# Splitting the weight slabs around a mixer by two transfers and a negation instead of by a subtraction on GpSimd

## The chip, the cores and the metric

The kernel runs on one core of one Trainium2 chip. The metric is the device time of one execution in microseconds (us); each kernel is executed several times and the median is compared. Engines are named as in the profile: PE is the matrix engine, PEld its weight loads, DVE the vector engine, ACT the scalar engine, POOL is GpSimd, and SP is the engine whose queue only starts transfers.

## The reference, cut to what matters

One layer in float32: a SwiGLU half-step, a mixer of two head groups (a gated convolution of width 31, and a linear recurrence), a second half-step, and a final norm, on 512 tokens of width 1024.

```
x = x + 1/2 * swiglu_ffn(rmsnorm(x), ffn1)        # 1024 -> 2816 -> 1024
x = x + hybrid_mixer(rmsnorm(x) @ w_in) @ w_out   # 1024 -> 2048, 1024 -> 1024
x = x + 1/2 * swiglu_ffn(rmsnorm(x), ffn2)
y = rmsnorm(x)
```

## The kernel before, in words

All large products run on PE in the type float32r. To keep the precision of float32, every operand is split into two float32r parts, hi (the value rounded) and lo (the value minus hi), and a product is three matmuls: hi times hi, hi times lo, lo times hi. The weights stream through as slabs of 128 partitions by 1024 columns (512 KB); there are 208 of them.

A slab passes through three stages, written as three functions. `slab_load` (L113) starts a transfer from SP's queue into a `raw` buffer (3 of them). `slab_hi` (L117) takes one of 5 buffers called `hl`, which hold both parts, and has ACT write the rounded copy (L119). `slab_lo` (L121) writes the lo part, raw minus hi (L133). It does so on DVE, or, for the slabs that are flagged `shared`, on POOL as long as a running estimate of POOL's work (`POOL_AHEAD`) is not over a limit: 72 of the 76 shared slabs go to POOL, 4 of them and the 132 others to DVE.

The program is a list of units, each the products on one slab. `run` (L159) goes through it; when it comes to the unit of slab n, it first emits the load up to slab n+5, the rounding up to n+3 and the lo part up to n+2 (`AHEAD`). A scheduler then places the instructions on the engines, and every engine takes its own in that order.

The units in order: gate and up products of the first half-step (weights stationary, 512 tokens, 24 matmuls a slab); its down products; the last 12 down slabs twice, for tokens 0 to 255 and then for 256 to 511 (`down_b_units`, two slabs of the first pass are kept for the second). Then the mixer: input products for half of the tokens at a time (`zc_units`, `rx_units`, `rg_units`, written to `pz`), the convolution as 248 operations on DVE (L503, L506), the recurrence (`lru`, L558), two multiplications of which are on POOL (L571, L590), a layer norm, and the output products (`out_units`). In between lie the gate and up products of the second half-step for tokens 0 to 255 (L712 to L716). All slabs from the second pass of the down products to these, 76 in number, are the shared ones. Each serves 256 tokens, so PE spends half as long on it as on a slab that serves 512. Before the units that need a new norm stands a `wait` (L679); the norm of two token tiles (`norm_chain`, L255) takes its sum of squares on ACT, two tiny operations on POOL (L218, L221), the scaling on DVE (L226), transposes on PE (L242), the rounding on ACT (L246) and the lo part on DVE (L252).

Of the kernel before, what the change touches and what calls it, by code (L numbers as in the profile page):

```python
# [8 lines left out]
F32 = mybir.dt.float32  # L9
F32R = mybir.dt.float32r  # L10
AF = mybir.ActivationFunctionType
ALU = mybir.AluOpType

P = 128
D = 1024
# [10 lines left out]
RAW_BUFS = 3  # L26
HL_BUFS = 5
ACT_BUFS = 19
AHEAD = (5, 3, 2)
POOL_CUT = 1  # L30
POOL_AHEAD = 1.0
DVE_AHEAD = 0.0
NY1 = 0
NY2 = 1
# [24 lines left out]
def layer_kernel(ctx: ExitStack, tc, x, gains, w_g1, w_u1, w_d1a, w_d1b, w_in,  # L59
                 chan, w_a, w_x, w_out, w_g2, w_u2, w_d2a, w_d2b, out):  # L60
    nc = tc.nc
    V, S, G, PE = nc.vector, nc.scalar, nc.gpsimd, nc.tensor

    cp = ctx.enter_context(tc.tile_pool(name="cp", bufs=1))
    wp = ctx.enter_context(tc.tile_pool(name="wp", bufs=4))
# [6 lines left out]
    def nm(s):  # L72
        uid[0] += 1
        return f"{s}_{uid[0]}"

    def const(shape, name, dt=F32):
        return cp.tile(shape, dt, name=name, tag=name)

# [1 line left out]
    xt = [const([P, D], f"xt{t}") for t in range(4)]  # L80
    h_hi = const([P, KT, T], "h_hi", F32R)
    h_lo = const([P, KT, T], "h_lo", F32R)
# [1 line left out]
    ones = const([P, P], "ones")  # L84
# [17 lines left out]
        nc.sync.dma_start(g, gains[i:i + 1, :].broadcast_to([P, D]))  # L102
        return g

# [1 line left out]
    clock = {"pe": 0.0, "dve": 0.0, "pool": 0.0}  # L106
    chains, convs, done = [], [], {}

    def dve(us):
        clock["dve"] = max(clock["dve"], clock["pe"] - 3.0) + us  # L110

    # slabs are loaded, then split into two parts of float32r
    def slab_load(st, src):  # L113
        st["raw"] = wp.tile([P, D], F32, name=nm("raw"), tag="raw", bufs=RAW_BUFS)
        nc.sync.dma_start(st["raw"], src)

    def slab_hi(st):  # L117
        st["hl"] = wp.tile([P, 2, D], F32R, name=nm("hl"), tag="hl", bufs=HL_BUFS)
        S.copy(st["hl"][:, 0, :], st["raw"])  # L119

    def slab_lo(st, shared):  # L121
        eng = V
        if shared:
            clock["pool"] = max(clock["pool"], clock["pe"])
            if clock["pool"] - clock["pe"] < POOL_AHEAD:
                eng = G
                clock["pool"] += 2.4
        if eng is V:
            dve(1.15)
        n = POOL_CUT if eng is G else 1  # L130
        for i in range(n):
            sl = slice(i * D // n, (i + 1) * D // n)
            eng.tensor_sub(st["hl"][:, 1, sl], st["raw"][:, sl],  # L133
                           st["hl"][:, 0, sl].bitcast(F32))

    def step_chains():
        for c in list(chains):
            with tc.high_priority(offset=c[0]):
                if next(c[1], None) is None:
                    chains.remove(c)  # L140

    def step_convs():
        while convs and clock["dve"] < clock["pe"] + DVE_AHEAD:
            with tc.high_priority(offset=PR_CONV):
                us = next(convs[0], None)
            if us is None:
                convs.pop(0)
            else:
                dve(us)
# [9 lines left out]
    def run(units, held):  # L159
        order = [i for i, x in enumerate(units) if x[0] is not None]  # L160
        st = [dict() for _ in order]
        put = [0, 0, 0]
        nth = 0
        for i, (src, shared, us, mm, evac) in enumerate(x[:5] for x in units):
            for stage, ahead in ((0, AHEAD[0]), (1, AHEAD[1]), (2, AHEAD[2])):
                most = HL_BUFS if i < held else len(order)
                while put[stage] < min(nth + ahead + 1, most):
                    q = put[stage]
                    if stage == 0:
                        slab_load(st[q], units[order[q]][0])  # L170
                    elif stage == 1:
                        slab_hi(st[q])
                    else:
                        slab_lo(st[q], units[order[q]][1])
                    put[stage] += 1
            hl = None
            if src is not None:
                hl = st[nth]["hl"]
                nth += 1
            mm(hl)  # L180
            clock["pe"] += us
            if us:
                step_chains()
                step_convs()
            if evac is not None:
                evac()

# [1 line left out]
    def mm_feat(ps, hl, t0, n):  # L189
        w = hl.rearrange("p s (k f) -> p s k f", k=KT)  # L190
        seq = [(0, h_hi), (0, h_lo), (1, h_hi)]
        for s, (a, h) in enumerate(seq):
            for k in range(KT):
                PE.matmul(ps, w[:, a, k, :], h[:, k, t0:t0 + n],  # L194
                          start=(s == 0 and k == 0), stop=(s == 2 and k == KT - 1))
# [5 lines left out]
            tc.keep_in_program_order(ins)  # L201
        return ins

    # a bank for the products beside the main ones
    def side_tile(name):
        if "free" in done:
            return pd.tile([P, T], F32, name=nm(name), tag="pd")
        return pp.tile([P, T], F32, name=nm(name), tag="pg")

# [1 line left out]
    def m4(name, dt=F32):  # L211
        return sp.tile([P, 4, HT], dt, name=nm(name), tag="act", bufs=ACT_BUFS)

# [58 lines left out]
        if key is not None:  # L272
            done[key] = True

# [1 line left out]
    def ffn_units(acts, j, wg, wu, parts, shared=False):  # L276
        box = {}

        def gate(t0, n, hl):
            if hl is not None:  # L280
                box["g"] = hl
            pg = pp.tile([P, T], F32, name=nm("pgate"), tag="pg")
            mm_feat(pg[:, :n], box["g"], t0, n)
            box["pg"] = pg

        def gate_out(t0, n):
            pg = box["pg"]
            sg = sp.tile([P, T], F32, name=nm("sg"), tag="sg", bufs=2)
            S.activation(sg[:, :n], pg[:, :n], AF.Silu)  # L289
            box["s"] = sg  # L290

        def up(t0, n, hl):
            if hl is not None:
                box["u"] = hl
            pu = pp.tile([P, T], F32, name=nm("pup"), tag="pg")
            mm_feat(pu[:, :n], box["u"], t0, n)
            box["pu"] = pu

        def up_out(t0, n):
            pu = box["pu"]  # L300
            sg = box["s"]
            act = acts[j]
            V.tensor_mul(sg[:, :n], pu[:, :n], sg[:, :n])  # L303
            S.copy(act[:, 0, t0:t0 + n], sg[:, :n])
            V.tensor_sub(act[:, 1, t0:t0 + n], sg[:, :n], act[:, 0, t0:t0 + n].bitcast(F32))  # L305
            dve(0.8 if n == 256 else 1.3)

        out_ = []
        for i, (t0, n) in enumerate(parts):
            us = 5.12 * n / 512  # L310
            out_.append((wg[j] if i == 0 else None, shared, us,
                         lambda hl, t0=t0, n=n: gate(t0, n, hl),
                         lambda t0=t0, n=n: gate_out(t0, n)))
            out_.append((wu[j] if i == 0 else None, shared, us,
                         lambda hl, t0=t0, n=n: up(t0, n, hl),
                         lambda t0=t0, n=n: up_out(t0, n)))
        return out_
# [6 lines left out]
            self[j] = new_act()  # L324
            return self[j]

# [1 line left out]
    def mm_tok(ps, ahi, alo, whi, wlo, first, last):  # L328
        PE.matmul(ps, ahi, whi, start=first, stop=False)  # L329
        PE.matmul(ps, ahi, wlo, start=False, stop=False)  # L330
        PE.matmul(ps, alo, whi, start=False, stop=last)  # L331
# [7 lines left out]
    def pd_tile():  # L339
        return pd.tile([P, 512], F32, name=nm("pd"), tag="pd")  # L340

    # down products of the first group of feature tiles, one half of the
    # output columns at a time, all tokens
    def down_a_units(wd, acts):
        box = {}

# [17 lines left out]
                 (lambda oh=oh: fin(oh)) if kp == NA // 2 - 1 else None)  # L364
                for oh in range(2) for kp in range(NA // 2)]

    # products of two token tiles with the full width of the output
    def pair_units(ws, order, kept, left, toks, scale, shared, after, again=False):
        box = {}
        n = len(order)  # L370
# [38 lines left out]
        order = [4, 5, 6, 7, 0, 1, 2, 3] if (YF0, YF1)[half] else list(range(8))  # L409
        return pair_units(w_out, order, {}, left, (2 * half, 2 * half + 1), 1.0, True, after)  # L410

# [1 line left out]
    def par(c, i):  # L413
        return ch[:, c, i:i + 1]

# [93 lines left out]
                    yield 0.4  # L509
        chains.append((PR_LN, layernorm(cv, half)))  # L510

    # mean over the channels, the same in every partition
    def channel_mean(v, box):
        ps2 = sp.tile([P, 2, HT], F32, name=nm("ps2"), tag="sg", bufs=2)
        V.tensor_add(ps2, v[:, 0:2, :], v[:, 2:4, :])
# [113 lines left out]
        V.tensor_scalar_mul(psp, q, 8.0)  # L629
        V.tensor_scalar_mul(nsp, q, -8.0)  # L630

# [1 line left out]
    row1 = sp.tile([1, P], F32, name="row1", tag="sg", bufs=2)  # L633
    V.memset(row1, 1.0)
    g1ps = [pd_tile() for _ in range(2)]
# [28 lines left out]
        return lambda: chains.append(  # L664
            (PR_NORM, norm_chain(toks, gains_of[n], f"h{n}{toks[0] // 2}")))

    # the same slabs once more, for the other half of the tokens
    def again_units(first, second):
        out_ = []
        for i, (_, _, us, mm, evac, _) in enumerate(second):  # L670
            box = {}
            first[i][5]["keep"] = box
            out_.append((None, False, us, lambda hl, mm=mm, box=box: mm(box.pop("hl")), evac))
        return out_
# [48 lines left out]
    for j in range(NB):  # L723
        u += ffn_units(b2, j, w_g2[NA:], w_u2[NA:], [ALL])

    # last down products and the final norm
    last = {}

    def final(k, hl):
# [100 lines left out]
```

## Time and profile before

| what | us |
|---|---|
| runs shown | 948.80 and 949.44, median 949.12 |
| span of the profiled execution | 945.9 |
| PE busy in the span | 907.8 |
| DVE busy | 475.1 |
| ACT busy | 368.6 |
| POOL busy | 210.8 |
| stretch 338 to 623 (the shared slabs): PE busy of 285 | 258.4 |
| the same stretch: DVE busy | 229.5 |

The span runs from the first to the last instruction of the profiled execution; it is 3.2 us shorter than the median of the runs, so the time of a kernel is read as its span and 3.2 us around it. A row of the groups gives the line, the engine, the operation, output and inputs by the program's names, shapes and count, then the total busy time, the mean in ns, and the idle time before. A row of a timeline gives start, duration, engine and instruction. A row of a table by stretches gives the length, then busy time and count of PE, PEld, DVE, ACT and POOL, then the granted PE clock, the share of the 16 transfer engines that is busy, and GB/s.

### The profile page before, as it was taken

To read this page: it belongs to the slowest core of one execution; us is meant where nothing else is said; L and a number is where in the kernel's file an instruction comes from. 1 tells how busy PE (TensorE), PEld (TensorE's weight loads), DVE (VectorE), ACT (ScalarE), POOL (GpSimd) and SP (SyncE) were. 2 spreads that over 40 slices of the span, in tenths; PEclk is the share of its full clock that TensorE was granted. 3 is DMA by queue.
4 is the path that set the end of the run, shared out by engine and by line. 5 is a ranking of instruction groups with operands and counts; after the bars stand their busy time and mean duration, and the time that the engine had idled before them with its cause. 6 is when DMAs were issued, how large, how long until landed. Compare 5 with 4: busy or idle time off the path is not lost.

```text
span 945.9 us, 11886 instructions
## 1 busy us (share of the span) xinstructions
PE 907.8 (96%) x4796; PEld 776.7 (82%) x4796; DVE 475.1 (50%) x677; ACT 368.6 (39%) x502; POOL 210.8 (22%) x120
## 2 busy tenths in 40 slices
PE   8999999999999999988889798999999999999997
PEld 6988888888888889888878697799988888888885
DVE  6533333333333433989999897555523333333224
ACT  6522221132222334466876554644511222223113
POOL 2000000000000038884856786700000000000001
PEclk9999999999999999998999899999999999999999
DMA  8322222322222344552433444445533222232202
GB/s 273 121 90 99 101 89 93 108 89 89 89 98 103 123 167 149 186 199 99 148 130 119 153 163 150 158 174 181 184 107 111 89 89 89 94 107 89 89 24 89
DMA packets 33401, 115.94 MB, mean 123 GB/s; under 512 B 4673, under 2 KB 4801, under 8 KB 33346
## 3 DMA queue, kind: packets, MB, share of 16 engines
q1 hardware_dynamic: 32770, 114.14, 34.8%
q10 hardware_dynamic: 576, 1.05, 0.3%
q8 instruction: 37, 0.61, 0.3%
q14 instruction: 18, 0.15, 0.0%
HBM read 113.07 MB, written 2.10 MB: 122 GB/s over the span
## 4 chain that ended last, share of the span: by engine, by line
PE 82%; DVE 13%; ACT 1%; DMA 1%; POOL 1%; issue 1%; SPq 0%; POOLq 0%; ACTq 0%; DVEq 0%
PE pgate L194 25%; PE pup L194 24%; PE pd L331 8%; PE pd L329 8%; PE pd L330 8%; PE pz L194 5%; DVE pc L506 4%; DVE xr L462 2%; PE pdl L331 1%; PE pdl L330 1%; PE pdl L329 1%; DVE th L595 1%; DVE xn L226 1%; DVE act L305 1%; DMA raw<-in_w_u 1%
## 5 line engine op out<-in xcount | busy, mean ns | idle before, releaser
L119 ACT CAST hl<-raw 128x1024 fp32r<-128x1024 f32 x208 | 217.7, 1048 | 330.6 <-PE pup L194 149.5
L133 DVE TENSOR_TENSOR hl<-raw,hl 128x1024 fp32r<-128x1024 f32 x136 | 168.2, 1237 | 290.3 <-ACT hl L119 290.3
L133 POOL TENSOR_TENSOR hl<-raw,hl 128x1024 fp32r<-128x1024 f32 x72 | 180.8, 2520 | 390.6 <-ACT hl L119 385.1
L194 PE MATMUL pgate<-h_hi,hl 128*128 128x512 f32 (+1 forms) x880 | 184.6, 352 | 0.8 <-ACT h_hi L246 0.8
L194 PE MATMUL pup<-h_hi,hl 128*128 128x512 f32 (+1 forms) x880 | 184.3, 351 | 0.3 <-DVE sg L303 0.3
L194 PEld LDWEIGHTS pgate<-h_hi,hl 128*128 128x128 f32 x880 | 145.0, 190 | 25.8 <-ACT h_hi L246 1.5
L194 PEld LDWEIGHTS pup<-h_hi,hl 128*128 128x128 f32 x880 | 144.9, 190 | 24.8 <-DVE sg L303 0.5
L329 PE MATMUL pd<-hl,act 128*128 128x512 f32 x304 | 118.4, 390 | 0.0
L331 PE MATMUL pd<-hl,act 128*128 128x512 f32 x304 | 118.3, 389 | 0.0
L330 PE MATMUL pd<-hl,act 128*128 128x512 f32 x304 | 118.3, 389 | 0.0
L506 DVE SCALAR_TENSOR_TENSOR pc<-ub,ch,pc 128x256 f32<-128x256 f32 x232 | 94.6, 477 | 0.0
L194 PE MATMUL pgate<-h_lo,hl 128*128 128x512 f32 (+1 forms) x440 | 92.3, 352 | 1.8 <-DVE h_lo L252 1.8
L194 PE MATMUL pup<-h_lo,hl 128*128 128x512 f32 (+1 forms) x440 | 91.7, 350 | 0.0
L289 ACT ACTIVATE sg<-pgate 128x512 f32<-128x512 f32 (+1 forms) x55 | 28.2, 513 | 159.0 <-PE pgate L194 159.0
L194 PEld LDWEIGHTS pgate<-h_lo,hl 128*128 128x128 f32 x440 | 72.5, 190 | 14.2 <-DVE h_lo L252 2.0
L194 PEld LDWEIGHTS pup<-h_lo,hl 128*128 128x128 f32 x440 | 72.1, 188 | 12.1
L303 DVE TENSOR_TENSOR sg<-pup,sg 128x512 f32<-128x512 f32 (+1 forms) x55 | 32.0, 583 | 94.6 <-PE pup L194 94.6
L758 POOL TENSOR_SCALAR sf<-sf 128x1 f32<-128x1 f32 x4 | 1.2, 300 | 323.7 <-ACT sqo L755 323.7
L194 PE MATMUL pz<-h_hi,hl 128*128 128x256 f32 x512 | 70.4, 287 | 0.0
L331 PEld LDWEIGHTS pd<-hl,act 128*128 128x128 f32 x304 | 57.1, 188 | 11.9
L329 PEld LDWEIGHTS pd<-hl,act 128*128 128x128 f32 x304 | 57.1, 188 | 11.8
L330 PEld LDWEIGHTS pd<-hl,act 128*128 128x128 f32 x304 | 57.1, 188 | 11.7
(118 smaller groups left out, 759.9 us busy)
## 6 DMA issues: line engine op xcount, KB each, us to landing
raw<-in_w_g SPq DMA_DIRECT2D x53, 512.0 KB, 3.2
raw<-in_w_u SPq DMA_DIRECT2D x53, 512.0 KB, 3.2
raw<-in_w_in SPq DMA_DIRECT2D x32, 512.0 KB, 3.2
raw<-in_w_d1b SPq DMA_DIRECT2D x22, 512.0 KB, 3.2
raw<-in_w_out SPq DMA_DIRECT2D x16, 512.0 KB, 3.2
raw<-in_w_d2b SPq DMA_DIRECT2D x12, 512.0 KB, 3.2
raw<-in_w_d1a SPq DMA_DIRECT2D x10, 512.0 KB, 3.2
raw<-in_w_d2a SPq DMA_DIRECT2D x10, 512.0 KB, 3.2
```

The costliest lines, as they stand in the source:

```text
L119: S.copy(st["hl"][:, 0, :], st["raw"])
L133: eng.tensor_sub(st["hl"][:, 1, sl], st["raw"][:, sl], st["hl"][:, 0, sl].bitcast(F32))
L194: PE.matmul(ps, w[:, a, k, :], h[:, k, t0:t0 + n], start=(s == 0 and k == 0), stop=(s == 2 and k == KT - 1))
L226: V.scalar_tensor_tensor(out=xn, in0=xt[t], scalar=ss[:, 1:2], in1=g, op0=ALU.mult, op1=ALU.mult)
L289: S.activation(sg[:, :n], pg[:, :n], AF.Silu)
L303: V.tensor_mul(sg[:, :n], pu[:, :n], sg[:, :n])
L305: V.tensor_sub(act[:, 1, t0:t0 + n], sg[:, :n], act[:, 0, t0:t0 + n].bitcast(F32))
L329: PE.matmul(ps, ahi, whi, start=first, stop=False)
L330: PE.matmul(ps, ahi, wlo, start=False, stop=False)
L331: PE.matmul(ps, alo, whi, start=False, stop=last)
L462: V.scalar_tensor_tensor(out=xr[:, c, :], in0=rxb[:, c, half * HT + k:half * HT + k + HT], scalar=par(c, P_LW + k), in1=xr[:, c, :], op0=A ...
L506: V.scalar_tensor_tensor(out=cv[:, c, :] if j == 30 else acc, in0=src, scalar=par(c, P_DW + j), in1=acc, op0=ALU.mult, op1=ALU.add)
```

## The change

The 76 shared slabs no longer have a `raw` buffer and no subtraction. `slab_load` takes an `hl` buffer at once and starts a transfer from POOL's queue that writes the rounded weights into its hi half (L117 of the changed kernel; source float32, destination float32r). `slab_hi` has ACT write minus hi into the lo half (L124). `slab_lo` starts a second transfer of the same weights from POOL's queue, which adds to what lies in the lo half (L131): minus hi plus weight. The other 132 slabs are loaded, rounded and subtracted as before, all on SP, ACT and DVE (L120, L127, L134). The loads of all slabs are emitted up to 4 slabs ahead instead of 5. With the casting load the `hl` buffer of a slab is taken at the load, 4 slabs ahead, not at the rounding.

```diff
-AHEAD = (5, 3, 2)
-POOL_CUT = 1
-POOL_AHEAD = 1.0
+AHEAD = (4, 3, 2)
...
-    def slab_load(st, src):
-        st["raw"] = wp.tile([P, D], F32, name=nm("raw"), tag="raw", bufs=RAW_BUFS)
-        nc.sync.dma_start(st["raw"], src)
+    def slab_load(st, src, shared):
+        st["src"], st["shared"] = src, shared
+        if shared:
+            st["hl"] = wp.tile([P, 2, D], F32R, name=nm("hl"), tag="hl", bufs=HL_BUFS)
+            G.dma_start(st["hl"][:, 0, :], src)
+        else:
+            st["raw"] = wp.tile([P, D], F32, name=nm("raw"), tag="raw", bufs=RAW_BUFS)
+            nc.sync.dma_start(st["raw"], src)
 
     def slab_hi(st):
-        st["hl"] = wp.tile([P, 2, D], F32R, name=nm("hl"), tag="hl", bufs=HL_BUFS)
-        S.copy(st["hl"][:, 0, :], st["raw"])
+        if st["shared"]:
+            S.mul(st["hl"][:, 1, :], st["hl"][:, 0, :].bitcast(F32), -1.0)
+        else:
+            st["hl"] = wp.tile([P, 2, D], F32R, name=nm("hl"), tag="hl", bufs=HL_BUFS)
+            S.copy(st["hl"][:, 0, :], st["raw"])
...
+    def slab_lo(st):
+        if st["shared"]:
+            G.dma_start(st["hl"][:, 1, :], st["src"], accum_op=ALU.add)
         else:
             dve(1.15)
...
+            V.tensor_sub(st["hl"][:, 1, :], st["raw"], st["hl"][:, 0, :].bitcast(F32))
```

What that does to the order is seen on POOL. The first place is its queue in the gate and up products of the second half-step for tokens 0 to 255, where one slab follows the other. Before, with `raw` and `hl` the buffers of one slab each:

```order
L133 TENSOR_TENSOR hl_4163<-raw_4089,hl_4163 128x1024 [waits DMAHW4_49,PE_49,Activation_49]
L133 TENSOR_TENSOR hl_4201<-raw_4122,hl_4201 128x1024 [waits DMAHW5_49,PE_49,Activation_49]
L133 TENSOR_TENSOR hl_4238<-raw_4161,hl_4238 128x1024 [waits DMAHW6_49,Activation_49]
L133 TENSOR_TENSOR hl_4278<-raw_4199,hl_4278 128x1024 [waits DMAHW7_49,PE_49,Activation_49]
L133 TENSOR_TENSOR hl_4314<-raw_4236,hl_4314 128x1024 [waits DMAHW0_49,Activation_49]
```

And the same place in the changed kernel:

```order
L117 DMA hl_4154<-in_w_g 128x1024 [waits DMASW6_49,DMASW1_49,PE_49]
L131 DMA hl_4078<-in_w_g 128x1024 [waits Activation_49]
L117 DMA hl_4189<-in_w_u 128x1024 [waits DMASW3_49,DMASW0_49,PE_49]
L131 DMA hl_4116<-in_w_u 128x1024 [waits Activation_49]
L117 DMA hl_4228<-in_w_g 128x1024 [waits DMASW5_49,DMASW2_49,PE_49]
L131 DMA hl_4154<-in_w_g 128x1024 [waits Activation_49]
```

One subtraction a slab has become two transfers a slab, in turn: a casting load, then the accumulating load of the slab two places earlier. The casting load waits for PE, which has to be done with the buffer's slab of five before; the accumulating load waits for ACT's negation.

The second place is POOL's queue at the norm of tokens 256 to 511 ahead of the mixer, whose statistics are `ss`. Before:

```order
L133 TENSOR_TENSOR hl_2900<-raw_2848,hl_2900 128x1024 [waits DMAHW2_49,Activation_49]
L218 TENSOR_SCALAR ss_2932<-ss_2932 128x1 [waits Activation_49]
L221 TENSOR_TENSOR ss_2932<-ss_2932,neghalf 128x1 [waits Pool_49]
L133 TENSOR_TENSOR hl_2950<-raw_2871,hl_2950 128x1024 [waits DMAHW3_49,Activation_49]
L218 TENSOR_SCALAR ss_2937<-ss_2937 128x1 [waits Activation_49]
L221 TENSOR_TENSOR ss_2937<-ss_2937,neghalf 128x1 [waits Pool_49]
```

In the changed kernel:

```order
L218 TENSOR_SCALAR ss_2908<-ss_2908 128x1 [waits Activation_49]
L117 DMA hl_2875<-in_w_in 128x1024 [waits DMASW5_49,DMASW2_49,PE_49]
L221 TENSOR_TENSOR ss_2908<-ss_2908,neghalf 128x1 [waits Pool_49]
L218 TENSOR_SCALAR ss_2913<-ss_2913 128x1 [waits Activation_49]
L131 DMA hl_2827<-in_w_in 128x1024
L221 TENSOR_TENSOR ss_2913<-ss_2913,neghalf 128x1 [waits Pool_49]
```

The statistics now stand behind a casting load that waits for a buffer, where they stood behind a subtraction.

More of the change, by code (lines that the diff above doesn't have):

```diff
@@ L110, in dve @@
         clock["dve"] = max(clock["dve"], clock["pe"] - 3.0) + us
-    def slab_load(st, src):
-        st["raw"] = wp.tile([P, D], F32, name=nm("raw"), tag="raw", bufs=RAW_BUFS)
-        nc.sync.dma_start(st["raw"], src)
-    def slab_hi(st):
-        st["hl"] = wp.tile([P, 2, D], F32R, name=nm("hl"), tag="hl", bufs=HL_BUFS)
[L119 to L128, printed above, removed]
-            dve(1.15)
[L130 to L134, printed above, removed]
+    def slab_load(st, src, shared):
[6 more added lines that the diff above has]
+            nc.sync.dma_start(st["raw"], src)
+    def slab_hi(st):
+        if st["shared"]:
[6 more added lines that the diff above has]
+            G.dma_start(st["hl"][:, 1, :], st["src"], accum_op=ALU.add)
+        else:
+            dve(1.15)
+            V.tensor_sub(st["hl"][:, 1, :], st["raw"], st["hl"][:, 0, :].bitcast(F32))
     def step_chains():
@@ L169, in run @@
                     if stage == 0:
-                        slab_load(st[q], units[order[q]][0])
+                        slab_load(st[q], *units[order[q]][:2])
                     elif stage == 1:
@@ L173, in run @@
                     else:
-                        slab_lo(st[q], units[order[q]][1])
+                        slab_lo(st[q])
                     put[stage] += 1
```

## The prediction

> **What bounds the kernel now.** I read the page first (busy times), then the busy times by stretch, then PE's waits, then single instructions.
>
> ```profile
> PE 907.8 (96%) x4796; PEld 776.7 (82%) x4796; DVE 475.1 (50%) x677; ACT 368.6 (39%) x502; POOL 210.8 (22%) x120
> 0.00:338.00 338.00, 333.26 (x1515) 272.81 (x1516) 127.44 (x159) 105.03 (x135) 6.44 (x20) 1.00 0.33 113
> 338.00:623.00 285.00, 258.41 (x1702) 237.26 (x1701) 229.53 (x383) 171.52 (x242) 200.88 (x92) 0.96 0.44 154
> 623.00:946.00 323.00, 316.14 (x1582) 266.59 (x1581) 118.17 (x136) 92.02 (x127) 3.44 (x8) 0.99 0.30 104
> ```
>
> PE bounds nearly everything. Its idle time lies in the middle stretch, which is also the only one where POOL works: 285.0 - 258.4 = 26.6 us. Before and after it PE misses 4.7 and 6.9 us at the two ends of the program. All 76 shared slabs fall into the middle, so the change can win at most these 26.6 us and what the granted clock of 0.96 costs there (some 10 us if PE got 1.00: 258.4 x 0.04).
>
> PE's waits between 330 and 640 us name who is late:
>
> ```profile
> PE pz L194 <- DVE h_lo L252: 6.0, 1, 6.0
> PE pm L521 <- DVE ps L516: 6.0, 3, 3.0
> PE ptr L242 <- DVE xn L226: 5.1, 2, 4.9
> PE pd L329 <- ACT uhi L549: 4.2, 2, 2.3
> ```
>
> It is DVE in three of four. And DVE there is slower than it need be:
>
> ```profile
> 414.42 2.40 POOL L133 TENSOR_TENSOR hl<-raw,hl 128x1024 fp32r<-128x1024 f32 x1
> 414.48 3.42 DVE L226 SCALAR_TENSOR_TENSOR xn<-xt,ss,gbc 128x1024 f32<-128x1024 f32 x1
> 416.97 3.17 POOL L133 TENSOR_TENSOR hl<-raw,hl 128x1024 fp32r<-128x1024 f32 x1 [0.15 <-ACT hl L119]
> 417.82 2.60 DVE L462 SCALAR_TENSOR_TENSOR xr<-rxb,ch,xr 128x256 f32<-128x256 f32 x1
> 423.74 0.47 DVE L462 SCALAR_TENSOR_TENSOR xr<-rxb,ch,xr 128x256 f32<-128x256 f32 x1
> 607.91 2.40 POOL L133 TENSOR_TENSOR hl<-raw,hl 128x1024 fp32r<-128x1024 f32 x1 [0.29 <-ACT hl L119]
> 611.30 1.28 DVE L226 SCALAR_TENSOR_TENSOR xn<-xt,ss,gbc 128x1024 f32<-128x1024 f32 x1 [1.16 <-POOL ss L221]
> ```
>
> The same scaling takes 3.42 us when a subtraction runs on POOL and 1.28 us after the last of them (POOL's last ends at 610.3); the same multiply-add takes 2.60 or 0.47. The difference of 2.1 us is nearly one POOL subtraction: DVE stands until POOL is done.
>
> **The change part by part: what goes.** 72 subtractions leave POOL and 4 leave DVE.
>
> ```profile
> L119 ACT CAST hl<-raw 128x1024 fp32r<-128x1024 f32 x208 | 217.7, 1048 | 330.6 <-PE pup L194 149.5
> L133 POOL TENSOR_TENSOR hl<-raw,hl 128x1024 fp32r<-128x1024 f32 x72 | 180.8, 2520 | 390.6 <-ACT hl L119 385.1
> L462 DVE SCALAR_TENSOR_TENSOR xr<-rxb,ch,xr 128x256 f32<-128x256 f32 x24 | 21.0, 902 | 0.0
> L226 DVE SCALAR_TENSOR_TENSOR xn<-xt,ss,gbc 128x1024 f32<-128x1024 f32 x8 | 18.7, 2340 | 5.6 <-POOL ss L221 5.6
> L133 DVE TENSOR_TENSOR hl<-raw,hl 128x1024 fp32r<-128x1024 f32 x9 | 12.7, 1408 | 2.4 <-ACT hl L119 2.4
> L305 DVE TENSOR_TENSOR act<-sg,act 128x256 fp32r<-128x256 f32 x8 | 8.4, 1051 | 1.1 <-ACT act L304 1.1
> L516 DVE TENSOR_TENSOR ps<-ps 128x256 f32<-128x256 f32 x4 | 7.2, 1806 | 0.0
> L595 DVE TENSOR_TENSOR_SCAN th<-r,hlast,xr 128x256 f32<-128x256 f32 x4 | 6.9, 1784 | 0.0
> L595 DVE TENSOR_TENSOR_SCAN th<-r,xr 128x256 f32<-128x256 f32 x4 | 2.4, 664 | 0.0
> ```
>
> POOL's 180.8 us go; the DVE rows are those in the stretch 338 to 623. With the undisturbed times (0.47 for L462 and the operations of its size, 1.28 for L226, 0.66 for a scan) the excess is 9.7 + 8.5 + 4.6 + 5.3 + 4.3 = 32 us, and the four subtractions of some 1.4 us make 6 more: DVE is relieved of about 38 us out of 229.5. That is more than PE's whole idle time, but PE's waits are also chains of ACT and POOL; I put what PE can win at 19 us of the 26.6, and bound it by 0 and 36 (all idle time and the clock).
>
> ACT's rounding becomes a negation of the same shape, 1.05 us a slab as before: nothing either way. It waits for the casting load now, and the evacuations of PE's results stand behind it in ACT's queue; that costs only if the loads are late.
>
> **What comes.** Two transfers of 512 KB a slab instead of one, both through the 16 transfer engines, and two issues on POOL. Rows for a plain transfer:
>
> ```profile
> q1 hardware_dynamic: 32770, 114.14, 34.8%
> raw<-in_w_in SPq DMA_DIRECT2D x32, 512.0 KB, 3.2
> 515.67 0.33 SPq L115 DMA_DIRECT2D raw<-in_w_g  x1
> ```
>
> 114.14 MB took 34.8% of 945.9 us, 329 us, so the engines move 347 GB/s and one slab (0.524 MB) keeps them busy for 1.51 us of the 3.2 us from issue to landing. The casting load I take at 1.51 us: it reads and writes as many bytes as a plain one. The accumulating load is not in the trace. From below it costs the same 1.51; it must however also read the 512 KB that lie in the buffer, and if an engine reads its two streams one after the other it is 2 x 1.51 = 3.02. I take 3.02, since the plain row already shows how long one stream of this size occupies the engines. A slab then costs 1.51 + 3.02 = **4.53 us of transfer**.
>
> Does other work hide it? Where the shared slabs lie on PE:
>
> ```profile
> 39.18 5.62 PE pgate L194 x24
> 356.62 0.88 PE ptr L242 x8
> 357.50 0.23 PE pd L329
> 612.27 2.85 PE pup L194 x24
> 621.43 1.11 PE L194 MATMUL pup<-h_hi,hl 128*128 128x256 f32 x8
> 622.38 2.03 PE L194 MATMUL pgate<-h_hi,hl 128*128 128x512 f32 x8
> ```
>
> PE starts the first of the 76 at 357.5 and is done with the last at 622.4: 265 us, 3.49 a slab, of which 2.8 are the slab's own products. 4.53 does not fit under 3.49, so the transfers become the bound. The 5 `hl` buffers fix the start: three shared slabs can be loaded early into free buffers, but the fourth needs the buffer of a kept slab, which PE leaves at 356.6. From there 73 slabs remain, and behind the last one stand the rest of a landing (3.2 - 1.5 = 1.7 us) and its products (2.8). PE is done at 356.6 + 73 x 4.53 + 1.7 + 2.8 = 691.8. Four transfers of 1.51 us that are not part of this (a gain, three `raw` slabs of what follows) share the engines at the end: 6.0 us, 697.8. That is 75.4 us after 622.4, and what follows is bound by PE as before, so it moves as a whole. Against the span of 945.9 this gives 1021.3, with the 3.2 us between span and median **1024.5**. DVE's relief is worth nothing in this sum, since the transfers run under it.
>
> The Trainium skill, page "DMA: Bandwidth & Descriptors", section "Where 436 GB/s comes from", puts the ceiling of the 16 ports at 435 GB/s. By that figure a pair would cost an estimated 3.6 us, PE would be done near 630 instead of 698, and the time would hardly change; the trace's 347 GB/s is the lower rate, and I go by it.
>
> POOL's two issues a slab are not in the trace either. From below they cost 0.33 us each, as SP's; from above one POOL operation that touches the same 128 x 1024, 2.5 us. I take 1 us, nearer to the issue, 2 us a slab: hidden under 4.53. At 2.5 each they would be 5.0 us a slab and POOL would be the bound.
>
> AHEAD 4 for 5 moves the plain loads one slab later; with 3.2 us to land and 5.6 us a slab in those stages, nothing.
>
> **The rivals.**
>
> *The two loads together stay under PE's pace, and DVE's relief shows.* If the accumulating load costs 1.51 us like a plain one, a slab costs 3.02, under 3.49; PE recovers 19 us: 949.1 - 19 = 930, between 913 and 940. For it speaks the contention shown above and that transfers are busy only 44% of the stretch; against it, that the added stream has to be read.
>
> *The loads just match the old pace.* The break-even is (622.4 - 1.7 - 2.8 - 356.6) / 73 = 3.58 us a slab, an accumulating load of 2.07 us. Between 3.3 and 3.85 a slab the time is 949 within 20 us; relief and loss cancel.
>
> *POOL's queue sets the pace.* At 2.5 us an issue a slab costs 5.0: 356.6 + 365 + 4.5 = 726, so 949.1 + 104 = 1053. What speaks for it is that each casting load waits in order for a free buffer and each accumulating load for ACT, with the norm's statistics (L218, L221) and the recurrence (L571, L590) queued behind; against it that an issue moves no data. The Trainium skill, page "SBUF — State Buffer", section "Who interferes with whom", adds that building descriptors for GpSimd's transfers is itself shut out while DVE uses both of its ports. No row here can show it, since no transfer leaves POOL before.
>
> *Casting is slow too.* If the conversion doubles the casting load as well, a slab costs 6.04 us: 356.6 + 441 + 4.5 = 802, 949.1 + 180 = 1129.
>
> *The change does not take place* is excluded: the order shows 152 transfers on POOL and no subtraction.
>
> **How the numbers follow.** Transfer-bound with an accumulating load of 2.6 to 3.6 us: 0.50, own range 994 to 1067 by the sum above (73 x 4.11 or 5.11). POOL's queue as the bound lies within the same range: 0.05. Relief shows: 0.22, of which 0.17 ends below 930. About even: 0.16. Slower transfers than all that: 0.07. The forecast is the likeliest, 1024.5. The range has to reach the faster case and the slow ones: 926 to 1066. Faster by over 2% (below 930): 0.17. Within 2%, about what a measurement of this kernel can tell from no change: 0.20, 0.15 of the even cases and the 0.05 left of the relief. Slower: 0.63, which is 0.50 + 0.05 + 0.07 and the last 0.01 of the even cases.
>
> **What would show it.** Right: the share of the transfer engines in the stretch of the shared slabs goes from 0.44 to 0.9 or more; PE's waits there name the accumulating load, L131; the pace of `pgate` and `pup` with 256 tokens goes from 2.8 to some 4.5 us; DVE's L226 shows 1.28 us everywhere. The forecast is wrong if the transfer engines have idle time there while PE doesn't wait for a slab (the accumulating load is cheap), or if POOL's issues stand back to back with the transfer engines idle.

## The result, and the profile after

The changed kernel took 992.63 us in the median (two runs, 991.53 and 993.74), beside 949.12 before: ratio 1.046, 95% interval 1.0434 to 1.0485. It is slower by 43.5 us; 75.4 were forecast.

The views below are those of the prediction, of the changed kernel. First the page's busy times, then the table by stretches. The middle stretch has been made longer, to 666, because the shared slabs now end there:

```profile
PE 923.7 (93%) x4796; PEld 780.0 (79%) x4796; DVE 432.1 (44%) x673; ACT 369.6 (37%) x502; POOL 138.5 (14%) x200
...
0.00:338.00 338.00, 332.82 (x1517) 272.31 (x1518) 127.36 (x159) 104.64 (x134) 6.85 (x21) 1.00 0.35 114
338.00:666.00 328.00, 274.29 (x1698) 240.75 (x1697) 184.64 (x377) 172.47 (x241) 128.20 (x172) 0.96 1.02 252
666.00:990.00 324.00, 316.62 (x1585) 266.99 (x1583) 120.08 (x138) 92.52 (x128) 3.44 (x8) 0.99 0.33 107
```

The first stretch and the last are as they were; everything happened in the middle. There the share of the transfer engines (the last but one number) went from 0.44 to 1.02 (over 1 where packets overlap), while DVE, whose lateness held PE up before, has 45 us less to do (184.6 for 229.5). Of PE's 43 us more in the middle, 27 are idle time (53.7 for 26.6). The other 16 are longer busy records of the same matmuls at the same clock, 0.96; their ends are modelled, so some waiting may be counted in them.

The end of the last shared slab, in PE's timeline, carries the whole change: 665.85 where it was 622.38, 43.5 us later. The fourth casting load of the shared slabs (the first of the two in its row) starts where the prediction put it (357.7; 356.6 forecast).

```profile
357.68 1.19 POOL L117 DMA_DIRECT2D hl<-in_w_in  x2
...
665.85 2.03 PE L194 MATMUL pgate<-h_hi,hl 128*128 128x512 f32 x8
```

PE's waits between 330 and 690 us (total, times, longest):

```profile
PE pz L194 <- DMA hl<-in_w_in: 24.9, 23, 2.9
PE pd L330 <- DMA hl<-in_w_out: 9.9, 8, 2.5
PE pd L330 <- DMA hl<-in_w_d1b: 5.8, 8, 1.8
PE pgate L194 <- DMA hl<-in_w_g: 3.9, 7, 0.9
PE pup L194 <- DMA hl<-in_w_u: 3.1, 6, 1.1
...
PE ptr L242 <- DVE xn L226: 0.8, 1, 0.8
```

The long waits on DVE (`h_lo`, `ps`, `xn`) are gone or under a microsecond; five waits on transfers into `hl` stand in their place, 47.6 us in all. They are spread over 52 places and none is over 2.9 us: not one stall, but a pace. Which of a slab's two loads it was is told by the view of the accumulating load's line (L131), in its list of who waited (us, times):

```profile
  PE pz L194: 24.9, 23
  PE pd L330: 15.8, 16
...
  PE pgate L194: 3.9, 7
  PE pup L194: 3.1, 6
```

The list of the casting load's line (L117) names ACT alone.

The page's transfer queues, transfer issues (last number: median us from issue to landing) and the negation's group:

```profile
q0 software_dynamic: 21888, 79.70, 32.8%
q1 hardware_dynamic: 21826, 74.29, 22.9%
...
hl<-in_w_in POOLq DMA_DIRECT2D x64, 512.0 KB, 7.6
raw<-in_w_g SPq DMA_DIRECT2D x44, 512.0 KB, 3.3
...
L124 ACT ACTIVATE hl<-hl 128x1024 fp32r<-128x1024 f32 x76 | 80.4, 1058 | 116.6 <-DMA hl<-in_w_in 35.9
```

Queue q0 holds the 152 new transfers: 32.8% of 989.7 us, 324.6 us, or 4.27 us of the engines' time for each of the 76 pairs (4.53 forecast). They queue for it: 7.6 us to land against 3.3 for a plain load in another stretch. ACT stands idle for 116.6 us just before its negations, 91.7 of them for loads into `hl`.

On POOL, each line's transfers of `in_w_in` (minimum, median and maximum ns) cost less of its time than assumed:

```profile
L117 POOL DMA_DIRECT2D hl<-in_w_in x32: 543/549/1126, 345.7 to 544.2; - x32
...
L131 POOL DMA_DIRECT2D hl<-in_w_in x32: 862/872/1204, 353.8 to 556.1; - x32
```

That is 0.55 + 0.87 = 1.4 us a slab, where 2 were taken.

### The profile page after: what moved, and what is told of

Its sections match the earlier page's. It is cut to its first block, busy times and chain, and to the rows that moved or that the text cites. A ratio compares the mean times of both kernels' runs of the same rounds, so it can differ in the third digit from the quotient of the medians.

```text
span 989.7 us, 11892 instructions
## 1 busy us (share of the span) xinstructions
PE 923.7 (93%) x4796; PEld 780.0 (79%) x4796; DVE 432.1 (44%) x673; ACT 369.6 (37%) x502; POOL 138.5 (14%) x200
## 3 DMA queue, kind: packets, MB, share of 16 engines
q0 software_dynamic: 21888, 79.70, 32.8%
## 4 chain that ended last, share of the span: by engine, by line
PE 70%; DMA 20%; issue 4%; POOL 3%; ACT 2%; SPq 0%; POOLq 0%; DVE 0%; ACTq 0%
PE pgate L194 23%; PE pup L194 23%; DMA hl<-in_w_in 7%; PE pd L330 7%; PE pd L331 6%; PE pd L329 6%; DMA hl<-in_w_out 4%; DMA hl<-in_w_g 4%; DMA hl<-in_w_d1b 3%; PE pdl L330 1%; PE pdl L329 1%; PE pdl L331 1%; POOL hl L117 1%; ACT hl L124 1%; POOL hl L131 1%
## 5 line engine op out<-in xcount | busy, mean ns | idle before, releaser
L134 DVE TENSOR_TENSOR hl<-raw,hl 128x1024 fp32r<-128x1024 f32 x132 | 161.6, 1225 | 290.7 <-ACT hl L127 290.7
L127 ACT CAST hl<-raw 128x1024 fp32r<-128x1024 f32 x132 | 138.3, 1048 | 283.3 <-PE pup L194 139.9
L194 PE MATMUL pgate<-h_hi,hl 128*128 128x512 f32 (+1 forms) x880 | 187.0, 354 | 5.4 <-DMA hl<-in_w_g 3.9
L124 ACT ACTIVATE hl<-hl 128x1024 fp32r<-128x1024 f32 x76 | 80.4, 1058 | 116.6 <-DMA hl<-in_w_in 35.9
L194 PE MATMUL pz<-h_hi,hl 128*128 128x256 f32 x512 | 74.6, 295 | 26.6 <-DMA hl<-in_w_in 24.9
L506 DVE SCALAR_TENSOR_TENSOR pc<-ub,ch,pc 128x256 f32<-128x256 f32 x232 | 94.0, 483 | 0.0
L194 PEld LDWEIGHTS pz<-h_hi,hl 128*128 128x128 f32 x512 | 66.6, 195 | 32.6 <-DMA hl<-in_w_in 29.6
```

The costliest lines, as they stand in the source:

```text
L124: S.mul(st["hl"][:, 1, :], st["hl"][:, 0, :].bitcast(F32), -1.0)
L134: V.tensor_sub(st["hl"][:, 1, :], st["raw"], st["hl"][:, 0, :].bitcast(F32))
L194: PE.matmul(ps, w[:, a, k, :], h[:, k, t0:t0 + n], start=(s == 0 and k == 0), stop=(s == 2 and k == KT - 1))
L506: V.scalar_tensor_tensor(out=cv[:, c, :] if j == 30 else acc, in0=src, scalar=par(c, P_DW + j), in1=acc, op0=ALU.mult, op1=ALU.add)
```

## The experiments

The theory to test: the 16 transfer engines set the pace, because the accumulating load costs more than a plain one, and DVE's relief is real but lies under them. Against it stand the chain (casting load, then negation, then accumulating load, in order on POOL and ACT, so that waiting, not work, sets the pace) and the shorter look-ahead. Ratios are to the kernel before, run on the same chip (medians 947.8 to 948.75).

**Without the accumulating load.** The lo halves then hold minus hi alone, so what comes out is not the layer's result.

```diff
-            G.dma_start(st["hl"][:, 1, :], st["src"], accum_op=ALU.add)
+            pass
```

> The changed kernel without its accumulating loads: the 76 shared slabs keep the casting load and the negation, so their lo half holds minus hi only and the outputs are not the reference's. Theory (the two transfers of a slab outrun PE's pace; the accumulating load is the dearer one): transfers fall to some 1.5 us a slab, the share of the transfer engines in the stretch of the shared slabs to about 0.45, PE no longer waits for slabs, and DVE's relief shows: 925 to 940 us. Rival (waiting in order on POOL and in ACT's queue for buffers and casting loads costs the 43 us, not the engines' time): the casting loads still wait for a buffer and ACT for them, so the time stays above 960 us.

Measured: 919.03 us, ratio 0.9701 (0.9682 to 0.972). The queue of the casting loads, their landing, the stretch 338 to 600 and DVE's scaling in this kernel:

```profile
q0 software_dynamic: 10944, 39.85, 14.1%
...
hl<-in_w_in POOLq DMA_DIRECT2D x32, 512.0 KB, 3.7
...
338.00:600.00 262.00, 258.17 (x1739) 237.56 (x1738) 184.44 (x382) 174.95 (x245) 59.07 (x96) 1.00 0.55 171
...
L226 DVE SCALAR_TENSOR_TENSOR xn<-xt,ss,gbc x8: 1262/1284/1286, 353.1 to 582.7; 128x1024 f32<-128x1024 f32 x8
```

PE misses 3.8 us of 262 and its clock is 1.00. The kernel before misses 26.6 in 285. So the relief, once nothing covers it, is worth 28.8 us, and all eight scalings on DVE take 1.28 us. A casting load occupies the engines for 14.1% of 917.2 / 76 = 1.70 us.

**The second load without its addition.** Number, order and waits of the transfers stay the same; the lo halves then hold the rounded weights, not the lo part.

```diff
-            G.dma_start(st["hl"][:, 1, :], st["src"], accum_op=ALU.add)
+            G.dma_start(st["hl"][:, 1, :], st["src"])
```

> The changed kernel with the second transfer as a plain casting load that overwrites the lo half (no addition; the outputs are not the reference's). Same number, order and waits of transfers. Theory (the added stream has to be read as well, so the accumulating load costs about 2.7 us and the casting load 1.5): two loads of 1.5 us make 3.0 us a slab, under PE's pace of 3.5, so the time falls to 930 to 950 us. Rival (both transfers from POOL's queue cost alike, some 2.1 us, through the conversion to float32r or the way POOL builds them): nothing changes, 985 to 995 us.

Measured: 941.38 us, ratio 0.9932 (0.991 to 0.9954). Its queue, the stretch 338 to 623 and PE's longest wait on a transfer:

```profile
q0 software_dynamic: 21888, 79.70, 26.1%
...
338.00:623.00 285.00, 263.41 (x1722) 237.21 (x1722) 186.84 (x381) 174.77 (x245) 101.77 (x171) 0.98 0.91 294
...
PE pz L194 <- DMA hl<-in_w_in: 5.4, 4, 2.3
```

The same 21888 packets and 79.70 MB, queued in the same way, cost 51 us less when nothing is added: the addition is what makes the changed kernel slower than the one before. The number of transfers, their order on POOL and their waits don't do that, but they aren't free. The kernel with the casting loads alone took 919.03 us, so of the 73.6 us between it and the changed kernel 22.4 come with the second transfer as such and 51.2 with its addition. PE still waits 13.0 us for transfers here. How much of the 22.4 is the engines' time (share 0.91) and how much the waiting in order was not separated. A load here occupies 26.1% of 939.7 / 152 = 1.61 us, so the accumulating one in the changed kernel took 4.27 less 1.61 to 1.70, that is about **2.6 us**, if the casting load costs there what it costs in these two kernels.

**The look-ahead alone**, in the kernel before.

```diff
-AHEAD = (5, 3, 2)
+AHEAD = (4, 3, 2)
```

> The kernel before with loads 4 slabs ahead instead of 5, the one part of the change that touches all slabs. Theory: a plain load lands in 3.2 us and a slab takes 2.8 us or more, so it costs nothing: 947 to 952 us. Rival (part of the 43 us comes from the shorter look-ahead): over 955 us.

Measured: 948.4 us, ratio 1.0005 (0.9986 to 1.0023). It costs nothing.

**Every second shared slab by transfers**, the others by ACT's rounding and POOL's subtraction.

```diff
...
-                        slab_load(st[q], *units[order[q]][:2])
+                        src_, sh_ = units[order[q]][:2]
+                        if sh_:
+                            nshared[0] += 1
+                            sh_ = "dma" if nshared[0] % 2 == 0 else "pool"
+                        slab_load(st[q], src_, sh_)
...
+        elif st["shared"] == "pool":
+            G.tensor_sub(st["hl"][:, 1, :], st["raw"], st["hl"][:, 0, :].bitcast(F32))
```

> Every second shared slab (38) is split by the two transfers, the other 38 as before by SP's load, ACT's rounding and POOL's subtraction. Theory (transfer engines are the bound at about 4.2 us a slab, and POOL's subtractions hold up DVE): transfers average (4.2 + 1.5) / 2 = 2.9 us a slab, under PE's 3.5, and half of DVE's waiting for POOL is gone: 935 to 945 us, faster than both kernels. Rival (POOL's in-order queue, where a subtraction or a casting load waits for PE or ACT and holds up what is behind it, is the bound): no better than the kernel before, 950 to 975 us.

Measured: 979.85 us, ratio 1.0348 (1.0325 to 1.037). It is 35 us above the theory's range and 5 above the rival's. Its queue, the stretch 338 to 623 and waits in 338 to 655:

```profile
q0 software_dynamic: 10944, 39.85, 17.5%
...
338.00:623.00 285.00, 244.35 (x1540) 220.85 (x1539) 184.32 (x361) 153.26 (x219) 154.60 (x123) 0.93 0.77 200
...
ACT hl L124 <- DMA hl<-in_w_in: 47.3, 13, 8.1
POOL hl L131 <- ACT hl L124: 45.4, 15, 7.6
...
PE pm L528 <- DVE ps L523: 11.1, 2, 6.2
```

A pair took 17.5% of 977.4 us / 38 = 4.50 us of the engines' time. The engines have time left (0.77) and PE is held up all the same. Half the pairs, then, don't give half the loss (32 us of 43.5). ACT waits up to 8.1 us for a casting load and POOL up to 7.6 for the negation, with other work behind both.

**No subtraction on POOL at all, three ways.** The first two take half or two thirds of the shared slabs by transfers and the rest on DVE; the third is the kernel before with all slabs on DVE.

```diff
...
+                            sh_ = nshared[0] % 2 == 0
...
+                            sh_ = nshared[0] % 3 != 0
...
-POOL_AHEAD = 1.0
+POOL_AHEAD = -1.0
```

> As the last mixed kernel, but the 38 shared slabs that are not split by transfers are subtracted on DVE, and POOL subtracts nothing; POOL's queue holds transfers, the two multiplications and the statistics alone. DVE gains 38 x 1.22 = 46 us of work over the 185 it had in the changed kernel and never stands behind a POOL subtraction. Theory now (the mixed kernel was slow because subtractions, casting loads and accumulating loads wait for each other in POOL's order): 930 to 950 us. Rival (the accumulating path itself is too long, ACT's queue stands at each negation until a casting load lands): 960 to 985 us, with ACT's waits on casting loads as long as in the mixed kernel.

Measured: 1004.91 us, ratio 1.0588 (1.0555 to 1.0621).

> Two of three shared slabs by the two transfers (51), one of three (25) on DVE, POOL subtracts nothing. Transfers average (2 x 4.27 + 1.5) / 3 = 3.35 us a slab, just at PE's pace of 3.4; DVE gains 31 us. Theory (transfer engines set the pace, POOL's order comes second): between half_dve and the changed kernel, 945 to 970 us. Rival (a negation that waits in ACT's queue is what costs, whatever the engines' share): about as slow as half_dve or slower than 975 us.

Measured: 1020.02 us, ratio 1.0754 (1.0729 to 1.0779). Both are slower than the changed kernel, which moves all 76 slabs, and the theory missed both. The first is 20 us above its rival's range too; the second is where its rival put it.

> The kernel before with POOL's subtractions all on DVE: 72 more at 1.22 us, 88 us of work for DVE, no transfer changed. Theory (DVE stands behind POOL's subtractions for some 32 to 45 us): DVE has 229 - 32 + 88 = 285 us of work in a stretch of 285, so it is the bound and the time rises by little: 950 to 975 us. Rival (the long DVE operations are slow for another reason and stay so): 229 + 88 = 317 us of DVE work, 980 us or more, with the scaling L226 still at 3.4 us in places.

Measured: 991.06 us, ratio 1.0444 (1.0415 to 1.0473). In this last one, the scaling, PE's longest wait and the stretch 338 to 680:

```profile
L226 DVE SCALAR_TENSOR_TENSOR xn<-xt,ss,gbc x8: 1279/1285/1287, 352.4 to 662.2; 128x1024 f32<-128x1024 f32 x8
...
PE pm L521 <- DVE ps L516: 58.1, 4, 34.4
...
338.00:680.00 342.00, 271.60 (x1772) 246.45 (x1771) 275.02 (x461) 178.88 (x250) 19.76 (x20) 0.90 0.41 133
```

The contention is confirmed: without POOL's subtractions the scaling takes 1.28 us eight times out of eight, with no new transfer in the program. The time is not what the theory gave, 16 us above its range. DVE isn't full (275 of 342 us), but PE waits 58 us for the sums of the layer norm, which come after the convolution in DVE's order. In the kernel with half of the slabs by transfers, the waits in 338 to 690 show the chain again:

```profile
POOL hl L131 <- ACT hl L124: 150.9, 31, 10.4
ACT hl L124 <- DMA hl<-in_w_in: 45.9, 14, 7.7
```

**The negation one slab later in ACT's order**, to give the casting load longer to land: in the changed kernel, in the one with every second slab by transfers and POOL's subtraction, and in the one with half of the slabs on DVE.

```diff
-AHEAD = (4, 3, 2)
+AHEAD = (4, 2, 2)
```

> The changed kernel with the negation placed one slab later in ACT's order (2 slabs ahead of use instead of 3), so that ACT stands less at negations whose casting load has not landed. Theory (the 16 transfer engines are full in this stretch, 4.27 us a slab): 985 to 998 us, the same as the changed kernel within 1%, though ACT's waits on casting loads fall. Rival (ACT standing at the negations delays everything behind it and is a large part of the 43 us): under 975 us.

Measured: 994.75 us, ratio 1.0479 (1.0446 to 1.0512). The time is the theory's, but ACT's waits for casting loads didn't fall as it had them: they are 104.4 us, where they were 91.7. The transfer engines are still full in its stretch 338 to 655:

```profile
338.00:655.00 317.00, 260.32 (x1581) 227.47 (x1580) 173.34 (x363) 161.48 (x224) 121.92 (x165) 0.96 1.00 247
```

> The mixed kernel (every second shared slab by transfers, the others subtracted on POOL) with the negation 2 slabs ahead instead of 3. There the transfer engines were not full (0.77), but ACT stood over 110 us at negations. Theory (in the mixed kernels ACT's and POOL's order is what costs): 945 to 965 us, clearly under its 980. Rival (something else in the mixture costs): 975 to 985 us.

Measured: 977.28 us, ratio 1.0299 (1.0258 to 1.0339).

> half_dve (every second shared slab by transfers, the others subtracted on DVE) with the negation 2 slabs ahead instead of 3. Theory, as for the other mixture: well under its 1005, 950 to 975 us. Rival: 995 us or more.

Measured: 1003.22 us, ratio 1.0569 (1.054 to 1.0599). In both mixed kernels the time stayed, so a place one slab later doesn't help. ACT's waits for casting loads stayed as well, 114.5 us for 112.5 in the first and 116.9 for 117.0 in the second, so what these waits cost was not tested. The row of the first of the two beside the 47.3 us above:

```profile
ACT hl L124 <- DMA hl<-in_w_in: 48.6, 14, 7.7
```

Its timeline (start, duration) shows a loop:

```profile
570.43 0.91 POOL L131 DMA_DIRECT2D hl<-in_w_u  x1 [3.04 <-ACT act L311]
...
571.03 0.89 POOL L117 DMA_DIRECT2D hl<-in_w_u  x1
...
577.26 1.06 ACT L124 ACTIVATE hl<-hl 128x1024 fp32r<-128x1024 f32 x1 [5.62 <-DMA hl<-in_w_u]
...
578.61 0.87 POOL L131 DMA_DIRECT2D hl<-in_w_u  x1 [4.27 <-ACT act L311]
...
579.42 0.63 POOL L117 DMA_DIRECT2D hl<-in_w_u  x1
```

The casting load goes out at 571.0, just behind an accumulating load, and its negation starts only at 577.3. The accumulating load follows at 578.6 and the next casting load behind it at 579.4: this turn takes 8.2 to 8.4 us.

**A sixth `hl` buffer and one more slab of look-ahead**, to loosen that loop, in the changed kernel and in the one with every second slab by transfers and POOL's subtraction.

```diff
-HL_BUFS = 5
-ACT_BUFS = 19
-AHEAD = (4, 3, 2)
+HL_BUFS = 6
+ACT_BUFS = 17
+AHEAD = (5, 3, 2)
```

> The changed kernel with 6 hl buffers instead of 5 and loads 5 slabs ahead (room is made by 17 instead of 19 activation buffers), so that each casting load is issued a slab earlier. Theory (the 16 transfer engines are full): no more than a few us are won, 980 to 998 us. Rival (the length of the loop from a free buffer through two landings to the next free buffer sets the pace): 6/5 of the slabs are in flight and the pace of 4.2 us falls towards 3.5, 950 to 970 us.

Measured: 988.99 us, ratio 1.0425 (1.0404 to 1.0446); its stretch 338 to 655:

```profile
338.00:655.00 317.00, 265.51 (x1627) 233.34 (x1626) 179.89 (x370) 167.87 (x233) 125.16 (x170) 0.96 1.02 254
```

With another buffer the engines are as full as ever and the time falls by under 4 us, while an accumulating load takes longer to land (median 9.1 us for 8.4): the changed kernel is bound by the engines' work, not by the length of the loop.

> The mixed kernel (every second shared slab by transfers, the others subtracted on POOL) with 6 hl buffers, loads 5 slabs ahead and 17 activation buffers. There the transfer engines are at 0.77 and the loop casting load, negation, accumulating load, free buffer holds only two slabs that go by transfers. Theory (that loop is what costs in the mixture): 945 to 965 us, under its 980. Rival (subtractions and transfers in one POOL queue, each waiting for ACT in turn): 970 to 990 us.

Measured: 970.38 us, ratio 1.0236 (1.0211 to 1.0262), 9.5 us below the same kernel with five buffers, but at the edge of the rival's range and above the theory's. Freer buffers and a longer look-ahead, for the slabs that POOL subtracts as well, are together worth those 9.5 us; the other 22 us above the kernel before stay unexplained. No kernel here that computes the whole layer is faster than the one before.

## Why the prediction was right, point by point, and where it was off

- **What bounds the kernel before: PE, held up by DVE, and DVE by POOL.** Right, and shown: with POOL's subtractions taken away, the scaling takes 1.28 us every time in two kernels (and seven times of eight in the changed one), and with only the casting load and the negation in their place PE's idle time in that part of the program falls from 26.6 us in 285 to 3.8 in 262. The relief was taken as 19 us; it is 28.8, of which the idle time makes 22.8, and the clock, 1.00 for 0.96, probably the rest. It lay between the bounds of 0 and 36. DVE itself was to be relieved of about 38 us; its busy time fell by 43, from 475.1 to 432.1.
- **The accumulating load costs about two plain streams.** The step on which the forecast rested, right in direction and too high: 2.6 us instead of 3.02. That its addition is the cost is shown, by the 51 us that the same load without it saves. That the cost is the reading of the old contents, as argued, is not shown; it might as well be the adding. The Trainium skill, page "DMA: Bandwidth & Descriptors", section "Where 436 GB/s comes from", has 435 GB/s for the ports, which the prediction quoted, and about 358 GB/s for what binds transfers between HBM and SBUF. With three streams of 0.524 MB a pair, the first gives an estimated 3.6 us and the second 4.4; 4.27 was measured, so the trace's own rate (4.53) was a better guide than the port figure.
- **The transfers become the bound.** Right: share 1.02, PE waits on little else (5.7 us beside 47.6), and more look-ahead or a later negation moves the time by under half a per cent.
- **The sum.** 32 us too high, and that splits by the timeline. From the fourth casting load at 357.7 to PE's end at 665.9, less 4.5 us for the last landing and its products, lie 303.7 us, so 73 slabs came at 4.16 us each. 4.53 instead of 4.16 is 27.0 us; the four other transfers, put at 6.0 at the end, are counted here within that pace; the start was 1.1 us later. 27.0 + 6.0 - 1.1 = 31.9. How the 33 us split between the pace and those four is not shown: with 6.0 us for them the pace would be 4.08. In the pair the casting load was a little dearer (1.6 to 1.7 for 1.51) and the accumulating one cheaper, which is the term that was mis-sized. The result lies just below the own range of this case (994 to 1067), since its lower bound, too, had the 6.0 us in it.
- **The relief is worth nothing in the sum.** Right in effect: it is 28.8 us with the casting load alone, 6.4 with a second load that adds nothing, and gone with the accumulating one. This is where the change's gain went: from waiting on DVE to waiting on transfers.
- **POOL's issues, 2 us a slab, hidden.** Right: 1.4 us, in a stretch in which POOL works 128 of 328 us.
- **ACT's negation for nothing, unless the loads are late.** The loads were late: ACT idled 91.7 us for them. What that cost is not shown. With the negation later in ACT's order the time was the same within the intervals, but ACT's waits were no shorter.
- **The rivals.** That the two loads stay under PE's pace is what happens without the addition: 3.2 us a slab, under the break-even of 3.58. Even then the time is 941.4, just above that rival's 913 to 940, since a second transfer took most of the relief. POOL's queue and a doubled casting load are excluded by the 1.4 and the 1.6 to 1.7 us.
- **The marks named beforehand.** The share came, and so did the waits on the accumulating load, which the view of L131 names. The pace came in part: it is 4.16 us over the 73 slabs, but in the gate and up products, for which some 4.5 was named, it is 3.85 (eleven slabs between these two rows, each the first matmuls that need the slab's lo half):

```profile
575.90 1.21 PE L194 MATMUL pgate<-h_hi,hl 128*128 128x256 f32 x8 [0.63 <-DMA hl<-in_w_g]
...
618.29 1.21 PE L194 MATMUL pup<-h_hi,hl 128*128 128x256 f32 x8 [1.09 <-DMA hl<-in_w_u]
```

The last mark came but for one: of the eight scalings in the changed kernel, seven take 1.28 us and one 3.40, beside one of POOL's two remaining multiplications (L590), as shown below.

What is open: why kernels with fewer transfers, and transfer engines that are not full, are still slower than the one before. The loop of casting load, negation and accumulating load may be part of it, since a sixth buffer and a longer look-ahead took off 9.5 of 32 us; the rest was not settled.

## What to carry to other kernels

Before work is moved from an engine to the transfers, compare what the new transfers of a slab occupy the engines with the time between two slabs: here 4.2 us against 3.5 decided it, though the engines were only 44% busy before. A pair that fits isn't free either: without the addition, at 3.2 us a slab, 22 of the 28.8 us of relief were lost. An accumulating load is not a plain one in price; measure it once with the addition taken out. And moving half of the work need not bring half of the effect: the six mixed versions, in which the moved half runs as a chain of load, operation and load through two engines' queues, all lost, for reasons that were settled only in part.

## What the runs showed of the hardware

An accumulating load of 512 KB into float32r occupied the transfer engines for about 2.6 us (worked out above), a casting load for 1.6 to 1.7, a plain one for 1.5. In the kernel with casting loads alone one took 3.7 us to land; in the changed kernel, with the engines full, the transfers into `hl` took 7.2 to 8.5 in the median, weight by weight.

An issue of a transfer on POOL did not hold DVE's scaling up; an operation on a large tile did. Two places of the changed kernel's timeline show it:

```profile
433.96 0.93 POOL L131 DMA_DIRECT2D hl<-in_w_in  x1
434.29 1.28 DVE L226 SCALAR_TENSOR_TENSOR xn<-xt,ss,gbc 128x1024 f32<-128x1024 f32 x1
...
553.13 2.68 POOL L590 TENSOR_TENSOR xr<-xr,th 128x1024 f32<-128x1024 f32 x1
553.50 3.40 DVE L226 SCALAR_TENSOR_TENSOR xn<-xt,ss,gbc 128x1024 f32<-128x1024 f32 x1 [1.71 <-POOL ss L221]
```

The same scaling takes 1.28 us beside an issue and 3.40 beside a multiplication. But POOL does not hold up every DVE instruction. Two lines of the kernel before have the same operation on the same shape. L462 has both its tile inputs in SBUF, the memory that holds the tiles; L506, the convolution, adds to `pc`, which the kernel keeps in PSUM, the memory that PE writes its results to (count, then minimum, median and maximum ns):

```profile
L506 DVE SCALAR_TENSOR_TENSOR pc<-ub,ch,pc x232: 399/476/484, 375.7 to 579.1; 128x256 f32<-128x256 f32 x116
...
L462 DVE SCALAR_TENSOR_TENSOR xr<-rxb,ch,xr x24: 470/472/2690, 417.8 to 498.4; 128x256 f32<-128x256 f32 x24
```

L462 takes up to 2.69 us, while none of the 232 of L506 takes over 0.48, though POOL works 200.9 of the 285 us of that stretch. So DVE's largest piece of work was never held up by POOL, and the relief lies in the other instructions. The Trainium skill, page "SBUF — State Buffer", section "Who interferes with whom", says that a DVE instruction with two inputs in SBUF contends with a GpSimd instruction that reads SBUF, and not with one that only writes it. The slow rows agree with the first half of it; the row beside the issue fits the second half only if an issue reads no SBUF, which no run here shows.
